# Turning the first two feed-forward blocks on TensorE, and splitting x a bank at a time

## The chip, the cores and the metric

The kernel runs on one core of a Trainium2 chip. The metric is the device time of one execution in microseconds (us); a kernel's figure is the median of its runs. Engines are named as the profile names them: PE is TensorE (PEld its weight loads), DVE is VectorE, ACT is ScalarE, POOL is GpSimd, SP is SyncE, whose queue issues nearly all DMAs.

## What is computed

Two layers of a decoder over 256 tokens of width 1024, all in float32. The part that matters here is the SwiGLU feed-forward step, which stands twice in each layer, and the norm ahead of every step.

```python
def rms_norm(x, g):
    xf = x.astype(jnp.float32)
    y = xf * lax.rsqrt(jnp.mean(xf * xf, axis=-1, keepdims=True) + EPS)
    return (y * g.astype(jnp.float32)).astype(x.dtype)

def swiglu(x, w_gate, w_up, w_down):
    return (jax.nn.silu(x @ w_gate) * (x @ w_up)) @ w_down

h = h + 0.5 * swiglu(rms_norm(h, ffn1_norm), ...)   # w_gate, w_up: 1024 x 2816
u = rms_norm(h, mix_norm)                           # attention of two kinds, output projection
...
h = h + mixed @ w_out
h = h + 0.5 * swiglu(rms_norm(h, ffn2_norm), ...)
h = h + sigmoid(rms_norm(h, ple_norm) @ w_ple_gate) * (p_i @ w_ple_proj)
```

After two layers a last `rms_norm` gives the output.

## The kernel before

**Numbers in two parts.** A float32 matrix is split into a rounded part (names ending in h, type fp32r) and the remainder (names ending in l). A product is three matmuls (`mm3`, L254): high x high, high x low, low x high. Weights come from HBM in pieces of 128x1024 (`Unit.load`, L140; `raw` tiles in seven buffers), are rounded on ACT (L152) into `wh`, and the remainder `wl` is formed on DVE (L153); `wh` and `wl` have eight buffers each. A piece of the form with 512 columns serves two chunks of the inner dimension. `Seven` (L174) loads four pieces and forms the operands of a scheme with seven instead of eight block products: sums on DVE (L188), then parts (L193, L194).

**Feed-forward step** (`ffn`, L531). The 2816 inner columns are six blocks: five of 512 and a last one of 256. For each block, gate and up products go to PSUM banks, one bank for each of two row blocks t of 128 tokens (48 matmuls of 512 columns for gate, 48 for up). `gated` (L534) applies Silu on ACT and multiplies on DVE (L540) into `pr`, 128 tokens by 512. In the very first step of the kernel, `ffn(..., feed=start)`, blocks are 0 (gate and up interleaved, weights in half pieces), 1, 2, 3, 4, 5, and block 3 is formed by `wide_seven` (L570): 7 operands x 2 halves x 3 matmuls, then two halves (`half_mm`) of 24 matmuls each. In the other three steps blocks 1 and 3 are of that form.

**Turning `pr`.** The down product needs `pr` with the inner columns on partitions. `Gates.add` (L496) does so in four moves: DVE turns 32x32 pieces in place (L502), a DMA stores the block in device memory (L504, `m`), four DMAs fetch it back in another order (L509, `ft`), and ACT and DVE split it (L516, L517). The columns of the gate and up weights are laid out on the host (`turned_order`, L39) so that the outcome is in place. For blocks 1 to 3, `sums` (L452) forms four combinations of the two turned row blocks (L469 to L472) and splits them (L476, L477).

**Order.** The program is written as one stream in which PE's work advances a clock of its own (`tick`, L239): a call of `soon(us, f)` puts a piece of work behind so many us of products. The round trip's fetch is put 2.5 us behind the store, and the split 7 or 8 us. Block 0's products are gated once block 1's gate products are written; the extra delay passed there (4.5) is not used by `add`. The framework that builds the program places each instruction in the queue of its engine, and that order can differ from the text's. Every queue runs in order: SP's holds the weight loads (L148, L185) and the round trip (L504, L509) alike.

**x.** The input of each step is `h`, turned to have its 1024 columns on partitions in eight chunks of 128, scaled by the norm's gain and split (`turn_h`, L365). For each half row block, four transposes on PE (L371) fill one PSUM bank `xt`; then `split` (L300), four times: ACT scales and rounds a chunk of 128x128 from PSUM (L305), DVE scales again and subtracts (L306), also from PSUM. There are seven such passages between steps, of four banks each; they stand at some 186, 293, 470, 490, 677, 783 and 961 us of the profiled execution. The very first x is loaded, already turned, and does not go through `turn_h`.

PSUM has eight banks of 128x512 that all names share in rotation; the scratch tiles `w0` to `w3` have two buffers each.

Of the kernel before, what the change touches and what calls it, by code (L numbers as in the profile page):

```python
# [33 lines left out]


BACK, PARTS = 2.5, 7.0


def turned_order(n):  # L39
# [25 lines left out]
def trunk(ctx: ExitStack, tc: tile.TileContext, xT, xr, pT, w, gains, fgain, consts, out):  # L65
# [48 lines left out]
    def after(later, earlier):  # L114

        tc.add_manual_dep(later.ins, earlier.ins.name, mybir.DependencyInfo(mybir.DependencyClass.NoSync, mybir.DependencyReason.DATA), reason="order")
# [12 lines left out]
    class Unit:  # L129


        def __init__(self, nk, cols=None, sub=1, cut=1, again=None):
            self.u = at[0] if again is None else again.u
            at[0] += again is None
            self.cols = cols or UNIT // nk
            self.per = max(1, PIECE // self.cols)
            self.sub, self.cut = sub, cut
            self.parts, self.here = {}, set()
# [122 lines left out]
    def both(x, *ix):  # L261
        return tuple(t[ix] for t in x)
# [32 lines left out]
    def in_runs(x):  # L295

        return x.rearrange("p j (a s) -> p j a s", s=32)


    def split(x, src, c, gcol, name, ts=slice(0, T)):  # L300

        xh, xl = x
        g = g_sb[:, gcol : gcol + 1]
        return (
            nc.scalar.activation(xh[:, c, ts], src, AF.Copy, scale=g),  # L305
            nc.vector.scalar_tensor_tensor(xl[:, c, ts], src, g, xh[:, c, ts].bitcast(F32), op0=ALU.mult, op1=ALU.subtract),  # L306
        )
# [57 lines left out]
    def turn_h(x, t, n, gcol, name):  # L365

        a = bank(f"xt{t}{n}_{name}")
        behind = newest_mm[0]
        for j in range(4):
            c = 4 * n + j  # L370
            after(nc.tensor.transpose(a[:, j * P : (j + 1) * P], h[:, t, c * P : (c + 1) * P], ident), behind)  # L371
        for j in range(4):
            c = 4 * n + j
            split(x, a[:, j * P : (j + 1) * P], c, gcol + c, name, slice(t * P, (t + 1) * P))

    def column(r, name):

# [54 lines left out]
    class Gates:  # L432


        def __init__(self, tag):
            self.tag, self.f, self.s, self.turned = tag, {}, {}, {}

        def tile(self, i):
            if i not in self.f:
# [12 lines left out]
        def sums(self, i):  # L452

            a, b = self.turned[i, 0], self.turned[i, 1]
            lo, hi = (slice(None), slice(0, 2)), (slice(None), slice(2, 4))
            e = SEVEN.index(i)
            if e == 0:

                self.spare = tuple(x_p.tile([P, KC, T], F32R, tag=f"x{q}", name=f"sx{q}_{self.tag}") for q in "hl")
            if e < 2:  # L460
                homes = [[q[:, 4 * e + k].rearrange("p (a b) -> p a b", a=2) for q in self.spare] for k in range(4)]
            else:

                homes = [[q[:, 2 + k].rearrange("p (a b) -> p a b", a=2) for q in self.tile(NBLK - 1)] for k in range(2)]
                homes += [[q[:, 0:2, P:T] for q in self.tile(c)] for c in SEVEN[:2]]
            two = [wt("w3", f"sum{k}_{self.tag}_{i}") for k in range(2)]
            ss = [two[k // 2][:, k % 2].rearrange("p (a b) -> p a b", a=2) for k in range(4)]
            s1, s2, s3, s4 = (in_runs(s) for s in ss)
            nc.vector.tensor_tensor(s1, b[lo], b[hi], ALU.subtract)  # L469
            nc.vector.tensor_tensor(s2, s1, a[lo], ALU.subtract)  # L470
            nc.vector.tensor_tensor(s3, a[lo], b[lo], ALU.subtract)
            nc.vector.tensor_tensor(s4, s2, a[hi], ALU.add)  # L472
            if e < 2:
                for k in range(2):
                    sh, sl = (q[:, 4 * e + 2 * k : 4 * e + 2 * k + 2] for q in self.spare)
                    nc.scalar.activation(sh, two[k], AF.Copy)  # L476
                    nc.vector.tensor_tensor(sl, two[k], sh.bitcast(F32), ALU.subtract)  # L477
            else:
                for k, (sh, sl) in zip(ss, homes):
                    nc.scalar.activation(sh, k, AF.Copy)  # L480
                    nc.vector.tensor_tensor(sl, k, sh.bitcast(F32), ALU.subtract)
            self.s[i] = homes
# [13 lines left out]
        def add(self, i, t, pr, more):  # L496


            f = self.block(i)
            n = 4 if i < NBLK - 1 else 2  # L500
            name = f"{self.tag}_{i}{t}"
            nc.vector.transpose(pr, pr)  # L502
            m = mem_p.tile([P, 4, n * 32], F32, tag="turn", name=f"m_{name}")
            nc.sync.dma_start(m, pr.rearrange("p (q r) -> p q r", q=4))  # L504
            a = wt("w2", f"ft_{name}", 4, n * 32)

            def back():
                for q in range(4):
                    nc.sync.dma_start(a[32 * q : 32 * q + 32], m[:, q].rearrange("(a f) r -> f a r", a=4))  # L509

            def parts():
                self.turned[i, t] = v = a.rearrange("p a (j s) -> p j a s", j=n)

                ks = slice(2 if i in SEVEN and t else 0, n)
                fh, fl = (in_runs(q) for q in both(f, slice(None), ks, slice(t * P, (t + 1) * P)))
                after(nc.scalar.activation(fh, v[:, ks], AF.Copy), newest_wh[0])  # L516
                nc.vector.tensor_tensor(fl, v[:, ks], fh.bitcast(F32), ALU.subtract)  # L517
                if i in SEVEN and t:
                    self.sums(i)

            soon(BACK, back)
            soon(PARTS + t, parts)

    def seven_mm(banks, x_of, ops, first, last):

# [3 lines left out]
                mm3(banks[p], x_of(p, j), (wh[:, c], wl[:, c]), first(p) and j == 0, last(p) and j == 1, skip_group_check=True)  # L529

    def ffn(x, n, tag, gcol, between=None, feed=None):  # L531
        gates = Gates(tag)

        def gated(i, t, g, u, m=512):  # L534
            s = flat("w0", f"s_{tag}_{i}{t}")[:, :m]
# [566 lines left out]
def _weights(i):  # L1102

    import numpy as np

    def cols(w, m):

        return w[:, m].reshape(-1, P, len(m)).transpose(1, 0, 2).reshape(P, -1)

    ar = np.arange  # L1110
    units = []
    for L in range(DEPTH):

        def wide(w, m):

            units.extend(cols(w[k : k + 512], m) for k in range(0, DM, 512))

        def ffn(n):
            wg, wu, wd = (i[f"{n}_w_{s}"][L] for s in ("gate", "up", "down"))
            for j in range(NBLK - 1):  # L1120
                m = 512 * j + turned_order(512)
                if j in wide_sevens(L == 0 and n == "ffn1"):
                    units.extend(np.concatenate([cols(v[k : k + 256], m) for v in (wg, wu)], axis=1) for k in (0, 256))
                    units.extend(cols(v[512:], m) for v in (wg, wu))
                    continue
                wide(wg, m)
                wide(wu, m)
            m = DFF - 256 + turned_order(256)
            wide(np.concatenate([wg[:, m], wu[:, m]], axis=1), ar(512))

            def down(b):
                units.extend(cols(wd[k : k + 256], ar(DM)) for k in range(512 * b, min(512 * b + 512, DFF), 256))

            def seven(b):
                for k in (512 * b, 512 * b + 256):
                    units.append(np.concatenate([cols(wd[k : k + 256], ar(c, c + 512)) for c in (0, 512)], axis=1))

            down(0)
            down(NBLK - 1)
            for b in SEVEN:  # L1140
                seven(b)
            down(4)

        ffn("ffn1")
        wi = i["w_in"][L]
        rot = np.r_[32:64, 0:32]
        wide(wi, ar(1024, 1536))
        for m in (0, 512, 256, 768):
            units.append(cols(wi, ar(m, m + 256)))
        units.append(cols(wi, ar(1536, 1792)))  # L1150
        units.append(cols(wi, np.r_[1792:1920, 1920:1984, 1920 + rot]))
        uq = i["w_uq"][L]
        nope = np.concatenate([192 * h + ar(128) for h in range(4)])
        rope = np.concatenate([192 * h + 128 + ar(64) for h in range(4)])
        rotd = np.concatenate([192 * h + 128 + rot for h in range(4)])
        units.append(cols(uq, np.r_[nope, rope, rotd]))
        ukv = i["w_ukv"][L]
        kn = np.concatenate([256 * h + ar(128) for h in range(4)])
        u = np.zeros((P, UNIT), ukv.dtype)
        u[:, :1024] = cols(ukv, np.r_[kn, kn + 128])  # L1160
        units.append(u)
        for k in range(0, DM, 256):
            units.append(cols(i["w_out"][L][k : k + 256], ar(DM)))
        ffn("ffn2")
        units.append(cols(i["w_ple_proj"][L], ar(DM)))
        for m in range(0, DM, 512):
            wide(i["w_ple_gate"][L], ar(m, m + 512))
    return np.stack(units)
# [55 lines left out]
```

## Time and profile before

| | us |
|---|---|
| median of 3 runs (lowest, highest) | 1006.04 (1004.79, 1007.29) |
| the profiled execution | 1003.63 |
| its span | 1001.8 |
| PE busy in it | 981.6 (98%) |
| DVE busy | 861.9 (86%) |
| ACT busy | 635.7 (63%) |

The page's second part shows the span in 40 slices of 25 us (tenths busy), with the granted clock of PE and the rate of all DMAs:

```profile
PE   9998999999999999999999999999999999999996
DVE  6689999967679999799998998899676799989995
ACT  6746656848566566567676556567766755756664
PEclk9999999999999999999999999999999999999999
GB/s 302 302 252 202 302 231 188 230 257 175 98 127 108 268 224 274 197 259 194 262 105 264 229 272 213 212 249 210 274 106 106 126 174 251 267 240 204 222 187 43
```

A busy time that nearly fills the span marks the engine that bounds the whole; where it dips, another engine or a transfer has the say in that stretch. A row of a time view has the start, the time taken, the engine, the line of the program, the operation, the tile written and those read, the sizes, the count and, in brackets, how long the engine stood idle before it and what ended that.

### The profile page before, as it was taken

The numbers are of one execution on the slowest core, as the hardware profiler recorded it, in microseconds if no ns is written. First come the engines' busy times: TensorE is split into PE (matmuls) and PEld (weight loads), VectorE is DVE, ScalarE is ACT, GpSimd is POOL, SyncE is SP. The second block draws the span as 40 slices with busy tenths as digits, with TensorE's granted clock in tenths as the row PEclk, the third lists the DMA queues.
The fourth block names the chain that finished last, engine by engine and source line by source line (L and its number), as shares of the span: only waits on it lengthen the run. The fifth ranks groups of instructions, "written<-read, shape, count | busy, mean of one in ns | idle before, by whom it ended". The sixth has DMA issues, their size and how long they took to land.

```text
span 1001.8 us, 14087 instructions
## 1 busy us (share of the span) xinstructions
PE 981.6 (98%) x4888; PEld 824.2 (82%) x4888; DVE 861.9 (86%) x1218; ACT 635.7 (63%) x974; POOL 12.4 (1%) x13
## 2 busy tenths in 40 slices
PE   9998999999999999999999999999999999999996
PEld 7875888899888888887788888888998888888875
DVE  6689999967679999799998998899676799989995
ACT  6746656848566566567676556567766755756664
POOL 0000000000100000000000000002000000000000
PEclk9999999999999999999999999999999999999999
DMA  8876875675233778685737686676733357776651
GB/s 302 302 252 202 302 231 188 230 257 175 98 127 108 268 224 274 197 259 194 262 105 264 229 272 213 212 249 210 274 106 106 126 174 251 267 240 204 222 187 43
DMA packets 88055, 210.50 MB, mean 210 GB/s; under 512 B 14000, under 2 KB 35632, under 8 KB 87984
## 3 DMA queue, kind: packets, MB, share of 16 engines
q1 hardware_dynamic: 87552, 209.03, 62.1%
q8 instruction: 38, 0.62, 0.2%
q10 hardware_dynamic: 432, 0.57, 0.2%
q14 instruction: 33, 0.27, 0.1%
HBM read 196.98 MB, written 12.58 MB: 209 GB/s over the span
## 4 chain that ended last, share of the span: by engine, by line
PE 86%; DVE 5%; DMA 4%; ACT 3%; issue 1%; SPq 0%; ACTq 0%; DVEq 0%
DMA raw<-in_w 4%; PE p_b L256 3%; PE g_a L256 3%; PE p_b L257 3%; PE g_a L258 3%; PE g_a L257 3%; PE g_b L257 3%; PE g_b L258 3%; PE g_b L256 3%; PE p_b L258 3%; PE d_a L257 3%; PE d_a L258 3%; PE d_a L256 3%; PE p_a L257 3%; PE p_a L258 3%; PE p_a L256 2%
## 5 line engine op out<-in xcount | busy, mean ns | idle before, releaser
L153 DVE TENSOR_TENSOR wl<-raw,wh 128x1024 fp32r<-128x1024 f32 (+1 forms) x278 | 321.0, 1187 | 49.5 <-ACT wh L152 48.1
L152 ACT ACTIVATE wh<-raw 128x1024 fp32r<-128x1024 f32 (+1 forms) x278 | 278.5, 1031 | 103.2 <-DMA raw<-in_w 47.4
L193 ACT ACTIVATE wh<-raw 128x1024 fp32r<-128x1024 f32 x133 | 139.0, 1058 | 130.0 <-DVE raw L188 98.9
L194 DVE TENSOR_TENSOR wl<-raw,wh 128x1024 fp32r<-128x1024 f32 x133 | 159.4, 1216 | 11.1 <-ACT wh L193 10.4
L188 DVE TENSOR_TENSOR raw<-raw,raw 128x1024 f32<-128x1024 f32 x76 | 92.6, 1220 | 4.5 <-DMA raw<-in_w 2.4
L256 PE MATMUL d_a<-wh,fh_a 128*128 128x512 f32 x108 | 42.3, 391 | 0.0
L258 PE MATMUL d_b<-wh,fl_b 128*128 128x512 f32 x108 | 42.2, 391 | 0.0
L256 PE MATMUL d_b<-wh,fh_b 128*128 128x512 f32 x108 | 42.2, 391 | 0.0
L258 PE MATMUL d_a<-wh,fl_a 128*128 128x512 f32 x108 | 42.1, 390 | 0.0
L257 PE MATMUL d_b<-wl,fh_b 128*128 128x512 f32 x108 | 42.1, 389 | 0.0
L257 PE MATMUL d_a<-wl,fh_a 128*128 128x512 f32 x108 | 42.0, 389 | 0.0
L256 PE MATMUL g_a<-wh,x0h 128*128 128x512 f32 x80 | 31.1, 390 | 0.3 <-ACT x0h L305 0.3
L257 PE MATMUL g_a<-wl,x0h 128*128 128x512 f32 x80 | 31.0, 389 | 0.0
L258 PE MATMUL g_a<-wh,x0l 128*128 128x512 f32 x80 | 31.0, 389 | 0.0
L257 PE MATMUL u_a<-wl,x0h 128*128 128x512 f32 x64 | 25.2, 394 | 0.5 <-DVE wl L153 0.5
L256 PE MATMUL g_b<-wh,x_mix0h 128*128 128x512 f32 x64 | 25.1, 392 | 0.0
L256 PE MATMUL g_b<-wh,x_mix1h 128*128 128x512 f32 x64 | 25.1, 392 | 0.0
L256 PE MATMUL g_a<-wh,xe0h 128*128 128x512 f32 x64 | 25.0, 391 | 0.0
L258 PE MATMUL u_a<-wh,x0l 128*128 128x512 f32 x64 | 25.0, 390 | 0.0
L258 PE MATMUL g_a<-wh,xe0l 128*128 128x512 f32 x64 | 24.9, 390 | 0.0
L257 PE MATMUL g_a<-wl,xe0h 128*128 128x512 f32 x64 | 24.9, 389 | 0.0
L258 PE MATMUL g_b<-wh,x_mix0l 128*128 128x512 f32 x64 | 24.9, 389 | 0.0
(552 smaller groups left out, 2683.9 us busy)
## 6 DMA issues: line engine op xcount, KB each, us to landing
raw<-in_w SPq DMA_DIRECT2D x338, 512.0 KB, 5.1
m_a<-pr_a SPq DMA_DIRECT2D x20, 256.0 KB, 2.1
ft_a<-m_a SPq DMA_DIRECT2D x80, 64.0 KB, 2.7
m_b<-pr_b SPq DMA_DIRECT2D x20, 256.0 KB, 2.3
ft_b<-m_b SPq DMA_DIRECT2D x80, 64.0 KB, 2.9
raw<-in_w SPq DMA_DIRECT2D x16, 256.0 KB, 4.4
xin<-in_xT SPq DMA_DIRECT2D x4, 256.0 KB, 4.7
h<-in_xr SPq DMA_DIRECT2D x2, 512.0 KB, 8.0
```

The source lines that it names most:

```text
L152: nc.scalar.activation(wh[:, a], r[:, a], AF.Copy),
L153: nc.vector.tensor_tensor(wl[:, a], r[:, a], wh[:, a].bitcast(F32), ALU.subtract),
L188: nc.vector.tensor_tensor(self.raw[o], self.raw[a], self.raw[b], op)
L193: newest_wh[0] = nc.scalar.activation(wh, r, AF.Copy)
L194: nc.vector.tensor_tensor(wl, r, wh.bitcast(F32), ALU.subtract)
L256: nc.tensor.matmul(o, ah, bh, start=start, stop=False, **kw)
L257: nc.tensor.matmul(o, ah, bl, start=False, stop=False, **kw)
L258: newest_mm[0] = nc.tensor.matmul(o, al, bh, start=False, stop=stop, **kw)
```

## The change

There are two parts.

1. In the first step's blocks 0 and 1 (`moved` is false), `pr` is turned by four PE transposes into a PSUM bank, 1.3 us (row block 0) or 2.2 us (row block 1) of products behind the call, plus the extra delay, which is now used. The split reads that bank. For `sums` of block 1, half of the second bank is first copied by ACT into the scratch tile `s3`, and DVE's combinations read the copy in its place. The weights' columns of these two blocks keep their natural order. All other blocks are as before.
2. `turn_h` has ACT scale the four chunks of a bank into a float32 tile `f` (in `w2`), then makes one rounding of 128x512 on ACT and one subtraction of 128x512 on DVE, both from that tile.

```diff
+def moved(first, i):
+    return not first or i > 1
...
 def turn_h(x, t, n, gcol, name):
...
+        f = flat("w2", f"xf{t}{n}_{name}").rearrange("p (a b) -> p a b", a=4)
         for j in range(4):
-            c = 4 * n + j
-            split(x, a[:, j * P : (j + 1) * P], c, gcol + c, name, slice(t * P, (t + 1) * P))
+            c = gcol + 4 * n + j
+            nc.scalar.activation(f[:, j], a[:, j * P : (j + 1) * P], AF.Copy, scale=g_sb[:, c : c + 1])
+        xh, xl = both(x, slice(None), slice(4 * n, 4 * n + 4), slice(t * P, (t + 1) * P))
+        nc.scalar.activation(xh, f, AF.Copy)
+        nc.vector.tensor_tensor(xl, f, xh.bitcast(F32), ALU.subtract)
...
-            nc.vector.tensor_tensor(s1, b[lo], b[hi], ALU.subtract)
+            blo = b[lo]
+            if not moved(self.first, i):
+                blo = s3
+                nc.scalar.copy(s3, b[lo])
+            nc.vector.tensor_tensor(s1, blo, b[hi], ALU.subtract)
             nc.vector.tensor_tensor(s2, s1, a[lo], ALU.subtract)
-            nc.vector.tensor_tensor(s3, a[lo], b[lo], ALU.subtract)
+            nc.vector.tensor_tensor(s3, a[lo], blo, ALU.subtract)
...
+            def parts(v):
+                self.turned[i, t] = v
+                ks = slice(2 if i in SEVEN and t else 0, n)
+                fh, fl = (in_runs(q) for q in both(f, slice(None), ks, slice(t * P, (t + 1) * P)))
+                h1 = nc.scalar.activation(fh, v[:, ks], AF.Copy)
+                nc.vector.tensor_tensor(fl, v[:, ks], fh.bitcast(F32), ALU.subtract)
+                if i in SEVEN and t:
+                    self.sums(i)
+                return h1
+            if not moved(self.first, i):
+                def go():
+                    a = bank(f"ft_{name}")[:, : n * P]
+                    behind = newest_mm[0]
+                    for j in range(n):
+                        after(nc.tensor.transpose(a[:, j * P : (j + 1) * P], pr[:, j * P : (j + 1) * P], ident), behind)
+                    parts(in_runs(a.rearrange("p (a b) -> p a b", a=n)))
+                soon(1.3 + 0.9 * t + more, go)
+                return
             nc.vector.transpose(pr, pr)
...
-            soon(PARTS + t, parts)
+            soon(PARTS + t, lambda: after(parts(a.rearrange("p a (j s) -> p j a s", j=n)), newest_wh[0]))
...
-                m = 512 * j + turned_order(512)
+                first = L == 0 and n == "ffn1"
+                m = 512 * j + (turned_order(512) if moved(first, j) else ar(512))
```

The removed `parts` of `add` did the same as the new one; it only took its source from the fetched tile.

More of the change, by code (lines that the diff above doesn't have):

```diff
@@ L432, in trunk, with __init__ @@
     class Gates:
-        def __init__(self, tag):
-            self.tag, self.f, self.s, self.turned = tag, {}, {}, {}
+        def __init__(self, tag, first):
+            self.tag, self.first, self.f, self.s, self.turned = tag, first, {}, {}, {}
         def tile(self, i):
@@ L509, in back @@
                     nc.sync.dma_start(a[32 * q : 32 * q + 32], m[:, q].rearrange("(a f) r -> f a r", a=4))
[L511 to L519, printed above, removed]
             soon(BACK, back)
-            soon(PARTS + t, parts)
+            soon(PARTS + t, lambda: after(parts(a.rearrange("p a (j s) -> p j a s", j=n)), newest_wh[0]))
     def seven_mm(banks, x_of, ops, first, last):
@@ L531, in ffn @@
     def ffn(x, n, tag, gcol, between=None, feed=None):
-        gates = Gates(tag)
+        gates = Gates(tag, feed is not None)
         def gated(i, t, g, u, m=512):
@@ L1120, in ffn @@
             for j in range(NBLK - 1):
-                m = 512 * j + turned_order(512)
-                if j in wide_sevens(L == 0 and n == "ffn1"):
+                first = L == 0 and n == "ffn1"
+                m = 512 * j + (turned_order(512) if moved(first, j) else ar(512))
+                if j in wide_sevens(first):
                     units.extend(np.concatenate([cols(v[k : k + 256], m) for v in (wg, wu)], axis=1) for k in (0, 256))
```

## The prediction

> **What bounds the kernel now.** I read the page first, then the busy time by stages, then TensorE's own order in the stages that stand out, then SyncE's queue there.
>
> ```profile
> span 1001.8 us, 14087 instructions
> PE 981.6 (98%) x4888; PEld 824.2 (82%) x4888; DVE 861.9 (86%) x1218; ACT 635.7 (63%) x974; POOL 12.4 (1%) x13
> ```
>
> TensorE (PE) is the bound: 98% busy, so a change can give only what PE loses while others keep it waiting. The busy time in stages of 20 us (PE, its weight loads, VectorE = DVE, ScalarE = ACT, then the granted clock) shows where that is:
>
> ```profile
> 40.00:60.00 20.00, 20.00 (x90) 16.57 (x89) 12.12 (x14) 7.85 (x9) 0.00 (x0) 1.00 0.67 206
> 60.00:80.00 20.00, 16.97 (x66) 12.38 (x64) 19.16 (x28) 11.65 (x17) 0.00 (x0) 0.91 0.78 281
> 80.00:100.00 20.00, 16.90 (x69) 12.75 (x70) 19.90 (x25) 14.20 (x17) 0.00 (x0) 1.00 0.65 208
> ...
> 460.00:480.00 20.00, 17.51 (x85) 13.93 (x83) 18.73 (x40) 15.29 (x34) 0.00 (x0) 1.00 0.62 208
> ...
> 560.00:580.00 20.00, 20.00 (x90) 16.49 (x89) 19.96 (x27) 13.35 (x17) 0.00 (x0) 1.00 0.63 217
> ...
> 680.00:700.00 20.00, 19.18 (x129) 16.41 (x128) 18.89 (x39) 13.97 (x33) 5.70 (x1) 1.00 0.66 217
> ...
> 960.00:980.00 20.00, 19.45 (x94) 15.57 (x93) 19.02 (x41) 14.17 (x35) 0.00 (x0) 1.00 0.32 108
> ```
>
> The big loss is at 60 to 100 us, in the first step. DVE is full there, yet was only 12.12 of 20 us busy just before. PE's order in time gives the size of the loss: block 2's gate products start at 49.74, its up products at 60.62, block 3 at 72.32, block 4 at 101.88.
>
> ```profile
> 49.74 0.39 PE L256 MATMUL g_a<-wh,x0h 128*128 128x512 f32 x1
> 60.62 0.39 PE L256 MATMUL u_a<-wh,x0h 128*128 128x512 f32 x1
> 72.32 0.39 PE L256 MATMUL p_a<-wh,x0h 128*128 128x512 f32 x1
> ...
> 76.42 0.80 PE L257 MATMUL p_a<-wl,xsh_a 128*128 128x512 f32 x1 [1.98 <-DVE wl L194]
> 77.02 0.63 PE L258 MATMUL p_a<-wh,xsl_a 128*128 128x512 f32 x1
> 77.44 0.63 PE L256 MATMUL p_a<-wh,xsh_a 128*128 128x512 f32 x1
> ...
> 101.88 0.39 PE L256 MATMUL g_a<-wh,x0h 128*128 128x512 f32 x1
> ```
>
> The 48 products of block 2's gate take 10.88 us, 0.2267 each. At that pace the up products lose 11.70 - 10.88 = 0.82 us. Block 3 has 7 operands x 2 x 3 and two halves of 24, 90 products: 20.40 us at full pace, 29.56 taken, 9.16 lost (part of it after a gap, where products follow at 0.42 instead of 0.23 and the stage's clock is 0.91). Together **9.98 us**.
>
> Why is DVE late? Its work there is the rounding remainder of weights (L153, L194), and those came late:
>
> ```profile
> 59.40 1.06 ACT L152 ACTIVATE wh<-raw 128x1024 fp32r<-128x1024 f32 x1 [8.35 <-DMA raw<-in_w]
> 60.49 1.23 DVE L153 TENSOR_TENSOR wl<-raw,wh 128x1024 fp32r<-128x1024 f32 x1 [4.60 <-ACT wh L152]
> ```
>
> SyncE's queue (start, time for the group, line, count) and its waits up to 62 us (total, times, longest) say why:
>
> ```profile
> 22.84 5.32 SPq L148 DMA_DIRECT2D raw<-in_w  x5
> 37.46 0.92 SPq L504 DMA_DIRECT2D m_a<-pr_a  x2
> ...
> 43.77 1.32 SPq L148 DMA_DIRECT2D raw<-in_w  x3
> 51.94 1.14 SPq L504 DMA_DIRECT2D m_a<-pr_a  x2
> 53.19 0.38 SPq L148 DMA_DIRECT2D raw<-in_w  x1
> 54.02 5.59 SPq L509 DMA_DIRECT2D ft_a<-m_a  x8
> 59.66 0.91 SPq L148 DMA_DIRECT2D raw<-in_w  x2
> 60.61 1.89 SPq L185 DMA_DIRECT2D raw<-in_w  x4
> ...
> SPq L504 <- DVE pr_a L502: 15.3, 3, 8.4
> ```
>
> The weight loads share one in-order queue with the round trip of blocks 0 and 1. For 15.3 us the queue stands at a store that waits for DVE's transposes; from 45.1 to 59.7 it gets one weight load out, and block 3's four loads follow at 60.61 to 62.5. So the cause of the loss is the place of L504 and L509 in SyncE's queue, before it is DVE's speed.
>
> **The change, part by part.** *First two blocks on TensorE.* Gone: four L502 transposes of 0.685 us, four stores (L504), sixteen loads (L509). With them SyncE's 15.3 us of waiting goes, and loads run on until buffers are full. Added to PE: 2 blocks x 2 row blocks x 4 = 16 transposes. The kernel has this operation already, in the chain of waits four at 0.44 us:
>
> ```profile
> 186.36 0.44 PE xt_a L371 x4
> ```
>
> 16 cost 1.76 us, all on the bound, before 55 us. Do they wait for `pr`?
>
> ```profile
> 35.41 1.41 DVE L540 SCALAR_TENSOR_TENSOR pr_a<-u_a,hr_in,s_a 128x512 f32<-128x512 f32 x2 [1.45 <-ACT s_a L536]
> 49.26 1.43 DVE L540 SCALAR_TENSOR_TENSOR pr_a<-u_a,hr_in,s_a 128x512 f32<-128x512 f32 x2 [2.97 <-PE u_a L258]
> ```
>
> Block 0's is written by 36.8 and turned 5.8 us of products into block 1's up stage, which starts 10.9 us ahead of 49.74: at 44.6. Block 1's is written by 50.0 and 50.7, since DVE stood waiting for its product, and turned 1.3 and 2.2 us of products (51.1 and 52.4 by whole triples) behind 49.74. So I cost the wait at nothing; if DVE comes late by one 1.2 us remainder, it costs some 0.5 us. PE's queue is in order, so all of block 2's gate products would stand behind it. Other engines see the same splits, now from PSUM, plus one ACT copy of 128x256 (some 0.4 us, at a time when ACT was busy 7.85 of 20 us).
>
> By the Trainium skill ("TensorE: Matmul & The Clock Gate", Part 4: PE-mode transpose) one transpose takes about 275 ns in a kernel's context and does not count as busy for the clock; by that 16 would cost 4.4 us and could lower the clock. This trace's single instruction is as long, but four follow each other in 0.44 us, and the stage from 680, where such transposes stand too, shows clock 1.00: the measured spacing decides.
>
> What is late next?
>
> ```profile
> 61.63 0.68 DVE L517 TENSOR_TENSOR fl_a<-ft_a,fh_a 128x512 fp32r<-128x512 f32 x1
> ```
>
> DVE's 39.06 us of work in 60 to 100 must fit PE's new 31.3 us for the same products, so about 7.8 us must be done earlier, in DVE's 7.88 idle us of 40 to 60. Two things move there: block 1's remainder and sums (from 61.63 to 65.65, 4.0 us, which waited for the round trip; the last of them, L477, is quoted below), and three remainders of block 2's up weights at some 1.2 us (that at 60.49 is the first; they waited for the loads at 53.19 and 59.66). That is 7.6 of 7.8. In the second layer the same kind of stretch (560 to 580, with a block of this form in it) runs with PE at 20.00 and DVE at 19.96, so DVE can do it when loads are in time. I leave **1.0 us** of stall (bounds 0 and 5, the upper if only half moves).
>
> *x's parts by banks.* Per bank of four chunks, before: four scaled roundings on ACT and four subtractions on DVE, all from PSUM. After: four scalings on ACT, one rounding of 128x512 on ACT, one subtraction of 128x512 on DVE. Prices from pairs and single rows:
>
> ```profile
> 191.01 0.61 ACT L305 ACTIVATE x_a0h<-xt_a,g_sb 128x128 fp32r<-128x128 f32 x2
> 191.70 0.60 DVE L306 SCALAR_TENSOR_TENSOR x_a0l<-xt_a,g_sb,x_a0h 128x128 fp32r<-128x128 f32 x2
> 64.36 1.29 DVE L477 TENSOR_TENSOR sxl_a<-sum_a,sxh_a 128x512 fp32r<-128x512 f32 x2 [0.24 <-ACT sxh_a L476]
> 68.62 1.31 ACT L562 ACTIVATE xsh_a<-xsum_a 128x512 fp32r<-128x512 f32 x2
> ```
>
> A further scaled 128x128 costs 0.25 on either engine; a 128x512 about 0.6. So DVE saves 4 x 0.26 - 0.6 = 0.44 us per bank, ACT adds 0.5 to 0.6. Seven passages x 4 banks = 28 banks: DVE -12, ACT +16 us. Neither is the bound on average, so only lateness counts. The first chunk of a bank is now ready after all four scalings, the rounding and the wide subtraction: 3 x 0.25 + 0.52 + 0.34 = 1.6 us later. Queued behind the rounding on ACT are the next weight roundings, and DVE's remainders and PE wait for those. The passage into the second mixing step is the tightest:
>
> ```profile
> 679.91 0.39 PE L256 MATMUL v<-wh,x_a1h 128*128 128x512 f32 x1
> 680.46 0.37 ACT L305 ACTIVATE x_a1h<-xt_a,g_sb 128x128 fp32r<-128x128 f32 x1
> 681.43 0.50 PE L258 MATMUL v<-wh,x_a1l 128*128 128x512 f32 x1 [0.16 <-DVE x_a1l L306]
> ...
> 477.43 0.61 DVE L306 SCALAR_TENSOR_TENSOR x_b0l<-xt_b,g_sb,x_b0h 128x128 fp32r<-128x128 f32 x2 [0.46 <-ACT x_b0h L305]
> 479.95 0.50 PE L257 MATMUL e<-wl,x_b0h 128*128 128x512 f32 x1 [1.68 <-DVE wl L153]
> ```
>
> There the fourth scaling starts at 680.46 and is over by 680.7 (at 0.25), and the rounding would be over at 681.2, while PE starts on the first chunk at 679.91: about 1.3 us late, in place of the waits for the DVE part that are there now. In the passage into the gate-projection step, at 479.95, PE waits not for x but for a weight remainder (1.68 us) that stands behind small subtractions such as that at 477.43 on DVE; fewer of them let it go sooner, one rounding more on ACT lets it come later. Bounds: below, the 2.49 + 0.82 + 0.55 = 3.9 us that PE idles in the stages at 460, 680 and 960; above, 1.6 us at each of seven, 11 us. I take **+1.0 us**, nearest to the one late passage less a little relief.
>
> Sum: -9.98 + 1.76 + 1.0 + 1.0 = -6.2 us. The profiled execution took 1003.63 us (span 1001.8), so 997.4 for one like it; the median of the runs, 1006.04, lies 2.41 above it, which gives **999.8**.
>
> **The rivals.**
> *The stall only moves* (0.20). SyncE's queue is held at block 2's store instead, or DVE's queue orders the earlier work badly; DVE at 19.16 and 19.90 of 20 speaks for it, the second layer's 560 to 580 against it. With 5 us of stall left instead of 1: 1003.8.
> *The hand-offs go too* (0.12). ACT and DVE no longer take turns at one PSUM bank, DVE is 12 us lighter, and the idle 3.9 us at the passages go instead of 1.0 being added: 999.8 - 4.9 = 995. ACT's fuller queue speaks against it. The Trainium skill ("PSUM — Partial Sum Buffer", PSUM bank collisions raise a hardware error) states that two engines must not touch one bank at once, reads included, which would be why such turns are there; no run here shows the error.
> *Later x at each passage* (0.13), the one that ends slower: one mechanism, the 1.6 us by which a bank's first chunk is later. The first step's net gain is 9.98 - 1.76 - 1.0 = 7.2 us, so from 1.03 us a passage, over all seven, the change gains nothing; from 1.46 it is slower by over 3 us; at the full 1.6 us: 1006.04 - 7.2 + 11.2 = 1010. For it: ACT at 15.29 and 13.97 of 20 in such stages, and PE already waiting at 681.43. Against it: most passages have other products to run meanwhile.
>
> **How the numbers follow.** The forecast has 0.55; its own range is 998 to 1002.5. The range reaches down to 996, most of the way to the hand-off case, and up to 1004.5, past the moved stall; the slow case and a rest below are left out, about 0.2. A measurement tells 0.3% (3.0 us) from no change, so faster means under 1003.0: 0.53 of the forecast, 0.12, and half of the moved stall, 0.75. Same: 0.02, the other half 0.10, and 0.05 of the late passages: 0.17. Slower: 0.08.
>
> **What the changed kernel's profile should show.** No L502, store or round trip in the first 55 us; SyncE's wait for DVE's transposes first at block 2; block 3's loads out before 57 us; PE near 20.00 in the stages at 60 and 80, with clock 1.00; block 4's gate products starting at 93 to 96 us instead of 101.88; four transposes at about 0.44 us each time; DVE some 15 us less and ACT some 16 us more busy in total. It is wrong if PE still idles over 3 us between 60 and 95, if PE waits for the transposed `pr`, or if stages at 180, 290, 500, 680 and 790 lose over a microsecond each for x.

## The result, and the profile after

| kernel | median, us (lowest to highest) | ratio to before, 95% interval |
|---|---|---|
| before, in the same session | 1006.08 (1004.79 to 1007.29) | |
| after | 989.15 (988.9 to 989.71) | 0.9833 (0.9816 to 0.985) |

The change is faster by 16.9 us, where 6.2 were forecast; 989.15 lies 6.9 us below the lower end of the range. The profiled execution of after took 989.71 us. Its page begins:

```profile
span 987.9 us, 14025 instructions
...
PE 977.5 (99%) x4904; PEld 826.0 (84%) x4904; DVE 850.4 (86%) x1130; ACT 652.3 (66%) x1003; POOL 9.3 (1%) x13
PE   9999999999999999999999999999999999999996
```

PE has 16 instructions more and is busy for 4.1 us less, since matmuls that follow a gap are recorded as longer: in the prediction's rows the three from 76.42 on have 0.80, 0.63 and 0.63 us, where the others have 0.39. DVE lost 11.5 us and ACT gained 16.6 (forecast: 15 and 16). What matters is PE's idle time. The busy time of after by stages (length, then PE, PEld, DVE, ACT, POOL with their counts, PE's clock, DMA share, GB/s):

```profile
40.00:60.00 20.00, 20.00 (x98) 16.59 (x97) 19.47 (x22) 14.60 (x19) 0.00 (x0) 1.00 0.90 317
60.00:80.00 20.00, 20.00 (x90) 16.57 (x89) 19.96 (x27) 13.79 (x17) 0.00 (x0) 1.00 0.39 132
80.00:100.00 20.00, 20.00 (x89) 16.54 (x89) 19.29 (x27) 12.21 (x15) 0.00 (x0) 1.00 0.81 287
460.00:480.00 20.00, 20.00 (x99) 16.53 (x98) 17.73 (x29) 18.50 (x44) 0.00 (x0) 1.00 0.69 228
480.00:500.00 20.00, 19.67 (x93) 16.00 (x92) 17.74 (x25) 17.36 (x36) 0.00 (x0) 1.00 0.61 207
...
680.00:700.00 20.00, 20.00 (x169) 19.70 (x168) 12.06 (x12) 9.61 (x12) 1.06 (x1) 1.00 0.82 282
```

PE is full where it idled before, in the first step (60 to 100) and in the passages (460, 680) alike. The counts of the two rows at 460, 85 before and 99 after, can't be set against each other as they stand, since the stage of after holds part of one set more of four short transposes; p2_only below has a pair that can. All that PE still waits for in after (total, times, longest):

```profile
PE warm L104 <- POOL ones L100: 1.0, 1, 1.0
PE xt_e L377 <- DVE h L1075: 0.3, 1, 0.3
PE g_a L263 <- DVE wl L159: 0.2, 1, 0.2
```

So by these waits almost nothing is left to gain from others' lateness. The first step's mechanism shows in SyncE's queue of after (start, time for the group, line, count):

```profile
24.25 20.73 SPq L154 DMA_DIRECT2D raw<-in_w  x12
45.79 4.33 SPq L191 DMA_DIRECT2D raw<-in_w  x4
51.52 22.67 SPq L154 DMA_DIRECT2D raw<-in_w  x7
75.80 1.00 SPq L543 DMA_DIRECT2D m_a<-pr_a  x2
```

Twelve weight loads go out in one run, block 3's four (L191) start 14.8 us sooner than before, and the first store stands at 75.80, for block 2. In the chain of waits the new transposes take the time they were given, and PE's order in time shows block 4's gate products at 94.34 instead of 101.88:

```profile
45.74 0.44 PE ft_a L536 x4
46.86 0.44 PE ft_a L536 x4
52.76 0.44 PE ft_a L536 x4
54.59 0.44 PE ft_a L536 x4
```

```profile
94.34 0.39 PE L262 MATMUL g_a<-wh,x0h 128*128 128x512 f32 x1
```

### The profile page after: what moved, and what is told of

Read it like the earlier page. It is cut to its first block, busy times and chain, and to the rows that moved or that the text cites. A ratio compares the mean times of both kernels' runs of the same rounds, so it can differ in the third digit from the quotient of the medians.

```text
span 987.9 us, 14025 instructions
## 1 busy us (share of the span) xinstructions
PE 977.5 (99%) x4904; PEld 826.0 (84%) x4904; DVE 850.4 (86%) x1130; ACT 652.3 (66%) x1003; POOL 9.3 (1%) x13
## 4 chain that ended last, share of the span: by engine, by line
PE 91%; ACT 3%; DVE 3%; DMA 2%; issue 1%; SPq 0%; ACTq 0%; DVEq 0%
PE p_b L262 3%; PE p_b L264 3%; PE p_b L263 3%; PE p_a L262 3%; PE p_a L264 3%; PE p_a L263 3%; PE d_a L264 3%; PE d_b L262 3%; PE d_b L263 3%; PE d_a L263 3%; PE d_a L262 3%; PE d_b L264 3%; PE g_b L262 3%; PE g_b L263 3%; PE g_b L264 3%; PE g_a L264 2%
## 5 line engine op out<-in xcount | busy, mean ns | idle before, releaser
L159 DVE TENSOR_TENSOR wl<-raw,wh 128x1024 fp32r<-128x1024 f32 (+1 forms) x278 | 324.3, 1191 | 61.8 <-ACT wh L158 58.5
L158 ACT ACTIVATE wh<-raw 128x1024 fp32r<-128x1024 f32 (+1 forms) x278 | 281.9, 1038 | 109.0 <-DMA raw<-in_w 21.1
L263 PE MATMUL g_b<-wl,x_mix1h 128*128 128x512 f32 x64 | 25.0, 391 | 0.0
L263 PE MATMUL g_b<-wl,x_mix0h 128*128 128x512 f32 x64 | 25.0, 391 | 0.0
L262 PE MATMUL u_a<-wh,x0h 128*128 128x512 f32 x64 | 24.9, 392 | 0.0
```

The lines of the kernel that those rows point to most:

```text
L158: nc.scalar.activation(wh[:, a], r[:, a], AF.Copy),
L159: nc.vector.tensor_tensor(wl[:, a], r[:, a], wh[:, a].bitcast(F32), ALU.subtract),
L262: nc.tensor.matmul(o, ah, bh, start=start, stop=False, **kw)
L263: nc.tensor.matmul(o, ah, bl, start=False, stop=False, **kw)
```

## The experiments

Diffs are against the changed kernel unless it says "against before". Every median stands beside its own runs of the kernel before, whose medians were 1006.08 to 1007.05.

### Which part gave how much

**p1_only**: the first two blocks by TensorE, the old `turn_h`.

```diff
-        f = flat("w2", f"xf{t}{n}_{name}").rearrange("p (a b) -> p a b", a=4)
         for j in range(4):
-            c = gcol + 4 * n + j
...
+            c = 4 * n + j
+            split(x, a[:, j * P : (j + 1) * P], c, gcol + c, name, slice(t * P, (t + 1) * P))
```

> The new way of turning blocks 0 and 1, with x's parts as before. Additive theory: the first step's loss of 9.98 us goes and 16 transposes cost 1.76 us, so some 8 us less than before (998), and the stages at the three passages into the gate-projection and second mixing steps keep the 5 to 6 us that TensorE idles there. Rival: the gain at the passages comes from the earlier start of the first step (another place of the loads), then it shows here too and this kernel is near 992 or below.

**p2_only**: the new `turn_h`, all blocks by the round trip.

```diff
-    return not first or i > 1
+    return True
```

> x's parts by banks, all blocks turned by the round trip as before. Additive theory: block 4's gate products start at 101 to 102 us as before, TensorE's idle time at the later passages goes, 5 to 6 us less than before (1000 to 1001). Rival, x's parts do nothing by themselves: within 1 us of before, with waits at the passages as before. The prediction's own step (x later at the passages): 1 us slower than before.

p1_only took 997.07 us (ratio 0.9909, 0.9894 to 0.9924), p2_only 998.71 (0.9922, 0.9905 to 0.9938). Against 1006.53 that is -9.5 and -7.8 us, together -17.3: the two parts add up, and the second, to which the forecast gave +1.0, is nearly half of the gain. p2_only's stage at 460 shows what came with it, without anything else being changed. This stage has four sets of transposes in both kernels, so the counts can be compared: 98 where before had 85, 13 x 0.2267 = 2.9 us gained, more than the 2.49 us by which PE was idle.

```profile
460.00:480.00 20.00, 20.00 (x98) 16.46 (x97) 19.59 (x31) 14.96 (x38) 0.00 (x0) 1.00 0.67 227
```

**before_again**: a second profiled execution of the kernel before.

> The kernel before, unchanged, for a second profile. If the first profile (1003.63 us) lay low because the stall in the first step differs from run to run, block 4's gate products start later than 101.88 us here, by as much as the run is longer. If the extra lies elsewhere, that start is at 101.9 and a later stage is longer.

It took 1006.46 us with a span of 1004.7, 2.9 above the first one. In 60 to 100 us it makes 130 matmuls where after makes 178; the stages that were quoted ahead of the forecast make 135. The first row is before's, the second after's:

```profile
60.00:100.00 40.00, 34.20 (x130) 25.31 (x130) 37.64 (x50) 25.37 (x32) 0.00 (x0) 0.91 0.69 237
```

```profile
60.00:100.00 40.00, 40.00 (x178) 33.11 (x177) 39.25 (x53) 26.00 (x31) 0.00 (x0) 1.00 0.60 209
```

48 x 0.2267 = 10.9 us lost there, not 9.98: the execution on which the sum was made had lost about 1 us less than this one. Block 4's gate products start at 103.40 us, 1.5 later than 101.88; 0.8 of it was there at the start of block 2's (50.53 for 49.74). So about half of the 2.9 us lies ahead of block 4, and the rest in later stages.

### The first step: what held the loads

**q_only** (against before): blocks 0 and 1 keep the round trip, but their DMAs are issued on POOL's queue, so SyncE's holds only loads.

```diff
-            nc.sync.dma_start(m, pr.rearrange("p (q r) -> p q r", q=4))
+            eng = nc.gpsimd if self.tag == "a0" and i < 2 else nc.sync
+            eng.dma_start(m, pr.rearrange("p (q r) -> p q r", q=4))
...
-                    nc.sync.dma_start(a[32 * q : 32 * q + 32], m[:, q].rearrange("(a f) r -> f a r", a=4))
+                    eng.dma_start(a[32 * q : 32 * q + 32], m[:, q].rearrange("(a f) r -> f a r", a=4))
```

> The kernel before, with the stores and fetches of the first step's blocks 0 and 1 issued from GpSimd's queue in place of SyncE's; VectorE's transposes and all the bytes stay. If the place in SyncE's queue is the cause of the first step's loss: block 4's gate products start by 94 us instead of 101.88 and the kernel takes 996 to 998. If VectorE's transposes or the round trip's bytes are: 100 to 102 us and within 2 us of before.

1006.79 us (1.0, 0.9988 to 1.0012): nothing gained, and block 4's gate products start at 101.10. Yet SyncE's queue is as free as in after, and block 3's loads go out at 45.72:

```profile
22.75 22.87 SPq L148 DMA_DIRECT2D raw<-in_w  x12
45.72 9.19 SPq L185 DMA_DIRECT2D raw<-in_w  x4
```

The next in-order queues take over the wait. ACT stands for the fetch with weights in hand, DVE stands for ACT, and later PE stands 5.3 us for ACT's rounding of the sums of x that block 3's products read (ACT's and DVE's order in time, then PE's waits):

```profile
51.70 0.63 ACT L517 ACTIVATE fh_a<-ft_a 128x512 fp32r<-128x512 f32 x1 [6.21 <-DMA ft_a<-m_a]
```

```profile
52.37 0.69 DVE L518 TENSOR_TENSOR fl_a<-ft_a,fh_a 128x512 fp32r<-128x512 f32 x1 [4.47 <-ACT fh_a L517]
```

```profile
PE p_a L256 <- ACT xsh_a L563: 5.3, 1, 5.3
```

By way of DVE the wait reaches block 1 too: its store goes out at 58.52, where SyncE had sent it at 51.94. But the round trip is also slower in this run. Block 0's fetch is issued from 41.77 on (39.52 before), and a fetch lands 5.1 us after its issue in the median, where the same sixteen took 3.9 us before. How much of the wait is due to that was not separated.

**q_late** (against before): q_only, with the split of blocks 0 and 1 also written much later.

```diff
-            soon(PARTS + t, parts)
+            soon((PARTS if eng is nc.sync else 32.0 - 7.0 * i) + t, parts)
```

> As the run with GpSimd's queue, and ScalarE's split of the fetched blocks 0 and 1 set behind more weight roundings (parts at 32 and 25 us of products in place of 7). If the stall had moved from SyncE's queue into ScalarE's, where the split waited 6.2 us for the fetch with all weight roundings behind it, the first step now runs with 3 us of loss or less (60 to 100 us) and the kernel takes 997 to 1000, with VectorE's transposes and all bytes still there. If transposes or bytes are the cause, the first step loses 8 us or more as before.

1000.7 us (0.9947, 0.9931 to 0.9964): 5.7 us gained against its 1006.41, with all of DVE's transposes and every byte of the round trip still there. So most of the loss is due neither to these nor to the bytes, but to in-order queues standing behind the round trip's latency; in q_only, freeing one queue only handed the wait to the next. Not all came back: from the start of block 2's gate products to block 4's q_late takes 45.8 us (49.85 to 95.64), 3.6 more than the 42.2 that are left of before's 52.14 without its loss of 9.98. What holds these 3.6 us stays open, and the late split was not tried with the old place in SyncE's queue.

**block1** and **block0**: only one of the two blocks by TensorE, the new `turn_h` (the diff is block1's; block0 has `i > 0`).

```diff
-    return not first or i > 1
+    return not first or i != 1
```

> The changed kernel with block 1 alone turned by TensorE; block 0 goes by the round trip again. If block 0's wait in SyncE's queue is harmless because buffers are full then: 0.9 us less than the changed kernel for eight transposes fewer, 988.3. If it matters: a loss of 2 to 6 us between 40 and 100 us, 991 to 995.

> Only block 0 by TensorE, block 1 by the round trip, x's parts as in the changed kernel. The run with block 1 alone gave 991.9, so block 0's round trip costs 2.8 us beside none. If block 1's round trip has cover (it is issued after block 0's work and the loads ahead of it are out): 988 to 989, less 0.9 us for two sets of four transposes. If its fetch holds SyncE's loads as block 0's did: 992 to 997, with the loss at 60 to 100 us.

991.91 us (0.9856, 0.984 to 0.9873) and 992.37 (0.986, 0.9843 to 0.9876). Either block alone gives most of the gain, and either round trip left in costs about 3 us (2.8 and 3.2), though two sets of four transposes less save 0.9. In block0 the stall is the old one, smaller: the store of block 1 holds SyncE's queue in the middle of block 3's loads, and PE waits for ACT's rounding of the sums of x.

```profile
44.59 2.60 SPq L191 DMA_DIRECT2D raw<-in_w  x3
52.27 0.92 SPq L543 DMA_DIRECT2D m_a<-pr_a  x2
53.29 0.40 SPq L191 DMA_DIRECT2D raw<-in_w  x1
```

```profile
76.15 0.69 PE L262 MATMUL p_a<-wh,xsh_a 128*128 128x512 f32 x1 [2.44 <-ACT xsh_a L591]
```

### The passages: what gained 7.8 us

Three things differ in the new `turn_h`: DVE has less work, the work is batched, and DVE no longer reads the PSUM bank, which also ends the turns of ACT and DVE at it.

**sub_by_chunk**: DVE's one subtraction cut into four.

```diff
-        nc.vector.tensor_tensor(xl, f, xh.bitcast(F32), ALU.subtract)
+        for j in range(4):
+            nc.vector.tensor_tensor(xl[:, j], f[:, j], xh[:, j].bitcast(F32), ALU.subtract)
```

> The changed kernel, with the one subtraction of 128x512 cut into four of 128x128, so VectorE is as busy as before the change (0.26 us each, 28 banks: 12 us more than in the changed kernel) while it still doesn't read the bank. If the passages gained by a lighter VectorE, the 5 to 6 us there come back: 994 to 995. If they gained because ScalarE and VectorE no longer take turns at a bank, it stays within 1.5 us of 989.2.

**chunks_sbuf**: rounding and subtraction chunk by chunk in turn, from the scaled tile.

```diff
-        nc.scalar.activation(xh, f, AF.Copy)
-        nc.vector.tensor_tensor(xl, f, xh.bitcast(F32), ALU.subtract)
+        for j in range(4):
+            nc.scalar.activation(xh[:, j], f[:, j], AF.Copy)
+            nc.vector.tensor_tensor(xl[:, j], f[:, j], xh[:, j].bitcast(F32), ALU.subtract)
```

> The changed kernel, with rounding and subtraction chunk by chunk from the scaled tile: no bank is shared, VectorE as busy as before the change, ScalarE with eight instructions of 0.25 us a bank in place of five (0.5 us more a bank, 13 us in all). If ending the turns at a bank is all that counts: within 1.5 us of 989.2. If VectorE's time is what counts: 994 to 995. If ScalarE's queue now decides: above 995.

989.24 us (0.9831, 0.9817 to 0.9846) and 990.03 (0.9841, 0.9826 to 0.9855). Neither the width of the instructions nor the batching is what gained: with a source in SBUF, ACT and DVE can work chunk by chunk at no loss that stands out of the intervals.

**order_only**: the old eight instructions, all from PSUM, but ACT's four first and then DVE's four.

```diff
+        for j, c, k in cs:
+            nc.scalar.activation(xh[:, c, ts], a[:, j * P : (j + 1) * P], AF.Copy, scale=g_sb[:, k : k + 1])
+        for j, c, k in cs:
+            nc.vector.scalar_tensor_tensor(xl[:, c, ts], a[:, j * P : (j + 1) * P], g_sb[:, k : k + 1], xh[:, c, ts].bitcast(F32), op0=ALU.mult, op1=ALU.subtract)
```

> The changed kernel's blocks 0 and 1, but x's parts by the very instructions of the kernel before: ScalarE's four scaled roundings and VectorE's four scaled subtractions, all eight from the PSUM bank. Only their order differs: all four roundings first, then all four subtractions, so the two engines take the bank once each and not four times in turn. Theory A (the passages gained 7.8 us because the engines took turns at the bank): 989 to 992. Theory B (they gained because ScalarE's and VectorE's instructions became others, with the subtraction's source in SBUF): 997, as the run with the first half of the change alone. ScalarE's busy time should fall by some 10 us against the changed kernel, VectorE's rise by some 12.

**two_banks**: the old split in turns, the four chunks spread over two banks.

```diff
+        two = [bank(f"xt{t}{n}{k}_{name}") for k in range(2)]
...
+            v = two[j % 2][:, j // 2 * P : (j // 2 + 1) * P]
+            split(x, v, c, gcol + c, name, slice(t * P, (t + 1) * P))
```

> The changed kernel's blocks 0 and 1, with x's parts chunk by chunk as before, but a passage's four chunks spread over two PSUM banks in turn: ScalarE can round chunk 1 from the second bank while VectorE subtracts chunk 0 from the first. Theory A (turns at one bank): most of the 7.8 us comes, 990 to 993. Theory B (other instructions): 997. A third, that a bank more in use at each passage holds TensorE up, gives over 997, with waits of TensorE for a bank in the rows.

993.19 us (0.987, 0.9855 to 0.9885) and 993.34 (0.9877, 0.9859 to 0.9894): each gives some 3.8 us of the 7.9 between p1_only and after. Neither theory had foreseen half.

**sub_stt** and **psum_sub**: ACT as in the changed kernel; DVE makes four scaled subtractions, in sub_stt from the scaled tile `f` (times 1.0), in psum_sub from the PSUM bank (times the gain).

```diff
-        nc.vector.tensor_tensor(xl, f, xh.bitcast(F32), ALU.subtract)
+        for j in range(4):
+            nc.vector.scalar_tensor_tensor(xl[:, j], f[:, j], 1.0, xh[:, j].bitcast(F32), op0=ALU.mult, op1=ALU.subtract)
```

> The changed kernel with VectorE's one subtraction of a passage's bank cut into four scaled ones (by 1.0) of the kernel before's kind, still from the scaled tile in SBUF; ScalarE's work and the PSUM bank's holding are the changed kernel's. If the 4 us that order_only lacks against the changed kernel are VectorE's time (four at 0.346 us and not one at 0.686, 0.7 us a bank): 992 to 993.5. If they come from VectorE's reading the PSUM bank (held until its last subtraction, and read beside other users of PSUM): 989 to 990.

> The changed kernel with ScalarE's work as it is (four scaled copies, one rounding), but VectorE's four scaled subtractions take the PSUM bank as their source again, after ScalarE has done with it. It stands to sub_stt as PSUM to SBUF alone. If reading the bank is what costs: 992 to 993.5 here and 989 to 990 in sub_stt. If VectorE's time: both 992 to 993.5. If neither (ScalarE's rounding straight from the bank is what costs in order_only): both 989 to 990.

989.77 us (0.9829, 0.9814 to 0.9843) and 999.55 (0.9927, 0.991 to 0.9943): 9.8 us for the source of one operand (and for the factor, which is a constant in the one and a column of gains in the other), more than the whole part had gained, though psum_sub has no turns. The groups show that the instructions' own length is not enough: 112 of them at 284 and 344 ns differ by 6.7 us of DVE in all, even if PE had to wait for every one (sub_stt, then psum_sub):

```profile
L386 DVE SCALAR_TENSOR_TENSOR x_a1l<-xf_a,x_a1h 128x128 fp32r<-128x128 f32 x16 | 3.8, 284 | 0.0
```

```profile
L387 DVE SCALAR_TENSOR_TENSOR x_a1l<-xt_a,g_sb,x_a1h 128x128 fp32r<-128x128 f32 x16 | 4.9, 344 | 0.1
```

What differs besides is the order of the queues. The framework lays each engine's queue out while it builds the program, so an edit can also move instructions that it does not name. The table counts, in the order of PE's records in each trace, the matmuls that stand ahead of a bank's four transposes (those of `h` not counted), for the two banks of `x_b0` and of `x_a1` in the first half of the tokens. The expectations below leave 101 further matmuls ahead of these banks out, so 2268 here is 2167 there.

```
kernel          x_b0          x_a1         median us
after           2268, 2271    3150, 3153     989.15
sub_stt         2268, 2271    3150, 3153     989.77
order_only      2272, 2273    3150, 3153     993.19
p1_only         2279, 2280    3158, 3159     997.07
psum_sub        2279, 2280    3160, 3161     999.55
```

The slower kernels have the transposes later. Four more runs separate that place from the work on the bank.

**p1_only_pin**, **psum_sub_pin**, **order_only_pin**: the same kernels, with the first matmul written after a bank's transposes bound to follow them in PE's queue. All three then have 2268, 2271 and 3150, 3153.

```diff
+        if turned_last[0] is not None:
+            after(nc.tensor.matmul(o, ah, bh, start=start, stop=False, **kw), turned_last[0])
+            turned_last[0] = None
```

> The run with the first half of the change alone (x's parts chunk by chunk, in turn at the bank: 997.1), but the first matmul written after a bank's four transposes is bound to stand behind them in TensorE's queue. So they stand where the changed kernel has them (behind 2167, 2170 and 4455, 4458 matmuls, and not 2178, 2179 and 4466, 4467, to name the passages before the attention of each layer's second half). Theory O (what the passages gained is the place of the transposes in the queue, which the kernel's scheduler lays out): 989 to 991. Theory T (the turns themselves, as they run on the chip): 996 to 998, with TensorE waiting behind the transposes.

> psum_sub (999.6) with the same binding. Theory O: 989 to 991, since only the source of VectorE's subtraction is left that tells it from sub_stt (989.8). Theory T, here that VectorE's holding of the bank costs on the chip: 998 to 1000.

> order_only (993.2) with the same binding: ScalarE's four scaled roundings, then VectorE's four scaled subtractions, the transposes early. Theory O: 988.5 to 990.5, the changed kernel's time with some 12 us less on ScalarE. Theory T: 992.5 to 994.

**late_turn**: the changed kernel, with the transposes of three passages written later (both banks of `x_b0` behind 2280 matmuls, both of `x_a1` behind 3159).

```diff
-            soon(wait[f], lambda f=f: turn_h(x, t, f, gcol, tag))
+            late = {"b0": (2.5, 2.05), "b1": (2.5, 2.05), "a1": (1.82, 1.37)}.get(tag, (0, 0))[f] if t == 0 else 0
+            soon(wait[f] + late, lambda f=f: turn_h(x, t, f, gcol, tag))
```

> The changed kernel, with the transposes of three passages (x_b0, x_a1, x_b1, the first half of the tokens) written later by the 8 to 11 matmuls by which the kernel before has them later. Theory O: TensorE loses 1 to 3 us at each of the three (at 460 to 500, 660 to 700 and 940 to 970 us), 992 to 996 in all. Theory T: the work on the bank is the changed kernel's, so 989 to 990.

| | order as laid out | transposes bound early |
|---|---|---|
| turns at the bank (p1_only) | 997.07 | 998.46 (997.9 to 999.08) |
| ACT first, then DVE, all from PSUM (order_only) | 993.19 | 991.21 (990.98 to 992.04) |
| scaled tile for ACT, DVE from PSUM (psum_sub) | 999.55 | 992.75 (992.33 to 993.02) |

late_turn took 989.72 us (989.33 to 990.07). The expectations name two theories, O for the place of the transposes in PE's queue and T for the turns at the bank; neither holds alone. The place of the transposes by itself costs nothing: late_turn has them late and takes 0.6 us more, within the spread of the runs. With the turns, an early place gains nothing either. p1_only_pin and order_only_pin make the same instructions, with PE's transposes in the same place, and differ only in whether ACT and DVE take the bank in turn or once each: **7.25 us**. Not all of it belongs to the bank: in the profiled executions 1.35 us is there by block 4's gate products (95.25 and 93.90), long before the first bank of x, and PE waits 0.8 us for a weight remainder at 40.45 in p1_only_pin alone. That leaves about 6 us for the turns, which is also what p1_only has over order_only_pin (5.9). ACT's and DVE's queues are laid out anew with the turns, so this is the price of both together. ACT shows the turns on the chip: in p1_only_pin it stands 3.0 us for DVE inside this passage, in order_only_pin not at all (groups of x_b0's rounding, in this order):

```profile
L316 ACT ACTIVATE x_b0h<-xt_b,g_sb 128x128 fp32r<-128x128 f32 x16 | 5.4, 363 | 3.0 <-DVE x_b0l L317 2.9
```

```profile
L389 ACT ACTIVATE x_b0h<-xt_b,g_sb 128x128 fp32r<-128x128 f32 x16 | 4.5, 378 | 0.0
```

And DVE, which waits little itself, has the bank's four subtractions strung out between weight remainders. Its order in time for one bank, in p1_only_pin and then in order_only_pin, with the next residual into `h`:

```profile
465.08 0.34 DVE L317 SCALAR_TENSOR_TENSOR x_b0l<-xt_b,g_sb,x_b0h 128x128 fp32r<-128x128 f32 x1
...
465.78 1.22 DVE L159 TENSOR_TENSOR wl<-raw,wh 128x1024 fp32r<-128x1024 f32 x1
466.91 0.35 DVE L317 SCALAR_TENSOR_TENSOR x_b0l<-xt_b,g_sb,x_b0h 128x128 fp32r<-128x128 f32 x1
...
467.29 0.35 DVE L317 SCALAR_TENSOR_TENSOR x_b0l<-xt_b,g_sb,x_b0h 128x128 fp32r<-128x128 f32 x1
...
469.35 0.69 DVE L409 SCALAR_TENSOR_TENSOR h<-d_b,h 128x512 f32<-128x512 f32 x1
```

```profile
461.07 1.22 DVE L159 TENSOR_TENSOR wl<-raw,wh 128x1024 fp32r<-128x1024 f32 x1
...
462.28 1.22 DVE L159 TENSOR_TENSOR wl<-raw,wh 128x1024 fp32r<-128x1024 f32 x1
...
463.48 0.86 DVE L391 SCALAR_TENSOR_TENSOR x_b0l<-xt_b,g_sb,x_b0h 128x128 fp32r<-128x128 f32 x3
...
464.34 0.34 DVE L391 SCALAR_TENSOR_TENSOR x_b0l<-xt_b,g_sb,x_b0h 128x128 fp32r<-128x128 f32 x1
...
465.77 1.28 DVE L414 SCALAR_TENSOR_TENSOR h<-d_b,h 128x512 f32<-128x512 f32 x2
```

From the first subtraction to the end of the fourth it is 2.6 us in the one and 1.2 in the other, and the residual begins 4.3 us after the first subtraction in the one, 2.3 in the other. DVE does not stand idle in between: what lengthens the one is the weight remainders that its queue holds between the subtractions, where the other has them ahead of the bank. So DVE's share of the price comes from the order of its queue. What is late then is `h`, and with it the next transposes. PE's largest waits of p1_only_pin:

```profile
PE xt_b L382 <- DVE h L409: 4.3, 4, 1.9
PE xt_e L382 <- DVE h L1076: 2.1, 2, 1.7
```

Left are 2.1 us from order_only_pin (991.21) to after (989.15), and 3.0 from psum_sub_pin to sub_stt: in these DVE still reads PSUM, is longer at it and holds the bank longer, which was not taken apart. psum_sub's other 6.8 us, and 2.0 of order_only's, come with the order of the queues, for they go when the transposes are bound; which of the moved instructions cost them stays open, since the binding moves others on DVE and ACT along.

## Why the prediction was wrong

**The bound and the mechanism of the first step: right.** PE's idle time was where it was said to be and went. The claimed cause, the place of L504 and L509 in SyncE's queue, was not enough by itself: q_only took exactly these out of the queue and gained nothing, since ACT's queue then stood behind the same, there even longer, latency; q_late, with the split out of the way as well, gained 5.7 us. What the forecast left out is that the split (L516) is a second in-order wait on the same round trip.

**The price of the transposes: right.** Four took 0.44 us, four times, with the clock at 1.00 and no wait for `pr`, so 1.76 us in all. The 4.4 us estimated from the Trainium skill ("TensorE: Matmul & The Clock Gate", Part 4: PE-mode transpose), and a lower clock, did not show.

**The residual stall of 1.0 us (bounds 0 and 5): the lower bound came true.** DVE did the moved work earlier, busy 19.47 of 20 us in 40 to 60, where it had been 12.12, and PE lost nothing in 60 to 100. With the 10.9 us that the second execution lost in place of 9.98, the first step's net is 10.9 - 1.76 = 9.1, near the 9.5 that p1_only measured, where 7.2 were forecast: some 2 us of the miss.

**The step that failed is the term for x's parts at the passages**, taken at +1.0 us with a lower bound of -3.9: it measured -7.8. Two things were wrong in it. The sign came from the first chunk, 1.6 us later. It is later, by about 1 us at the first bank of `x_a1` (its rounding ends 3.3 us after the transposes begin at 664.22 in after, the first chunk's some 2.3 us after 676.73 in before), but PE waits for nothing of x in after. What had kept PE waiting in the passages before were mostly weight remainders on DVE:

```profile
PE e L257 <- DVE wl L153: 1.7, 1, 1.7
PE pv L257 <- DVE wl L153: 1.4, 2, 0.8
```

Both waits are gone in after and in p2_only. And the lower bound took PE's idle time in three stages of one execution, 3.9 us, as all there was to gain. Matmuls after a gap follow each other more slowly and count as busy: from the start of block 4's gate products to the end of the span p2_only takes 894.0 us, where that execution of before took 899.9, 5.9 more, and before_again 901.3.

**The rivals.** "The hand-offs go too" had the mechanism, and at 995 the right side, with a chance of 0.12 and a size capped by that same idle time. Its two halves, the turns and DVE's lighter load, were not equal: dropping the turns is worth about 6 us at one place of the transposes, with the new order of ACT's and DVE's queues in it, DVE's wide subtraction against four narrow ones (sub_by_chunk) nothing that can be measured. "The stall only moves" did not happen in the change, but it is just what q_only does. "Later x at each passage" did not happen.

**The offset.** Adding 2.41 us from the profiled execution to the median was sound: the second execution lay at 1006.46.

## What to carry to other kernels

Where two engines read one PSUM bank piece by piece in turn, price the turn and not the instructions: what costs is the work that the in-order queues hold behind it and the order in which they are laid out around it, and one engine should be done with the bank before the other starts, or copy it to SBUF once. When a wait on a round trip is taken out of one in-order queue, look for the next queue that waits for the same data before counting the gain. Bound what can be gained in a stage by the instructions done in it at full pace, not by the bound engine's idle time.

## What the runs showed of the hardware beside that

- A scaled 128x128 subtraction on DVE takes 284 ns from SBUF and 344 ns from PSUM (sub_stt and psum_sub). The factor differs too, a constant in the first and a column of gains in the second; the two were not separated.
- Issued on POOL's queue beside loads that run freely (q_only), the round trip's fetch landed 5.1 us after its issue in the median, against 3.1 for the later ones on SyncE's queue in that kernel and 3.9 for the same sixteen in the kernel before. Whether the queue or the loads made it slower was not tried.

```profile
ft_a<-m_a SPq DMA_DIRECT2D x64, 64.0 KB, 3.1
...
ft_a<-m_a POOLq DMA_DIRECT2D x16, 64.0 KB, 5.1
```
